# Splits, masks and bias work of a mixing layer moved from GpSimd to VectorE and ScalarE, and the input weights held in four smaller buffers

## The chip, the cores and the metric

The kernel runs on one core of a Trainium2 chip. The metric is device time in microseconds (us) of one launch, taken by a counter of the chip; a profiled execution of the same program gives the trace. The engines are named PE (TensorE, matmuls), DVE (VectorE), ACT (ScalarE), POOL (GpSimd) and SP (SyncE, which here issues most DMAs). PEld is the weight load of TensorE.

## The reference, cut to what matters

One layer on x of 256 tokens by 1024: a mixing sublayer and a top-4-of-32 mixture of experts, both with a residual and a layer norm.

```python
x = layer_norm(x, ln_in_w, ln_in_b)
p = x @ w_in                                   # 1024 x D_IN: columns of RWKV-7 (8 heads of 64) and GLA (4 heads)
p_rwkv = p_rwkv + (shift(p_rwkv) - p_rwkv)*mu   # mixes each token with the one before
decay, a, g = small two-step projections of p_rwkv
kk = k*k_k / norm(k*k_k);  k = k*(1 + (a - 1)*k_a)
S_t = S_{t-1}(diag(w_t) - kk_t (kk_t*a_t)^T) + v_t k_t^T ;  y_t = S_t r_t     # by chunks of 64 tokens
y = (groupnorm(y)*gn_w + gn_b + sum(r*k*r_k)*v) * g
o = gla_chunked(q, k, v, gk); o = rms(o)*norm_w * silu(g_gla)
x = layer_norm(alpha*x + concat(y, o) @ w_out)
# experts: 4 of 32 per token, blocks of rows sorted by expert
h = xt[tok] @ w1[e] + b1[e];  act = (clip(up) + 1)*min(gt, 7)*sigmoid(1.702*gt);  o = act @ w2[e] + b2[e]
x = layer_norm(alpha*x + sum_of_gated(o))
```

Matmuls of the mixing sublayer are to be as good as float32, so both operands are split into a high and a low part in TensorE's rounded float32 (fp32r), and three products are added.

## The kernel before, in words

The tokens lie in two tiles of 128. After the first layer norm, x is transposed and split into `xth` and `xtl`. The columns of `w_in` come in 14 blocks of up to 256 columns (8 KB in each partition); `load_win` issues each block's DMA on SP. Two blocks share one 16 KB buffer of the pool `ring` (tag `slot`, two buffers).

`split()` (lines 383 to 392) makes the two parts of a piece of 128x512 weights: `whi` by a ScalarE copy (L388), `wlo` by a subtract (L391) on the engine that is passed in, VectorE by default. `proj_t` (transposed output) and `proj_n` (output with tokens on partitions) then issue three matmuls for each weight tile (L401 to L403 in `proj_t`). The results lie in PSUM banks with the tag `p`, of which there are two. `shift` (L429 ACT, L430 DVE) takes a result out and mixes it with the token before; only then is its half of a bank free.

The order of work is found when the program is built: a scheduler places each instruction on its engine's queue by data dependence and a priority that follows the source order. Each engine then runs its queue in order, so an instruction that waits holds up all behind it.

From some 108 us on, the projections for GLA (`wqk`, `wgv`, `wgg`) run between the chunk algebra of RWKV: `scores` (L630), `inverse16` (L648 to L671: eight masked products `dgm`, L661, four by DVE from the high part and four by POOL from the low part, for each of two chunk pairs; then a serial loop of 15 steps of two small DVE instructions, L669 and L670), `doubling` (L692 to L698) and `rwkv_chunk`. POOL also scales the residual `xres` by the first norm's weight and bias (L378, four of 128x1024), multiplies the bonus term (L817) and prepares the expert bias `b1`: the 32x2048 bias lies four times on the 128 partitions and is taken apart into bf16 pieces, copy (L587), subtract (L589), copy (L590). The pieces `b1p` are the moving operand of the bias matmul L1314, with `e32b` picking the expert's row of each piece.

Then comes the out projection with `w_out`, the second norm, the router, and the experts. The expert stream has ten buffers of 16 KB: six `xp` (0 to 5, which earlier hold activations), two of `ring` ('a', the same as the two of `w_in`) and two of `ringb` ('b', opened when the pools of the mixing stage close). `fetch` issues the stream's DMAs on SP in the order given by `ORDER`, each when its buffer is free: four loads of `w_out` of 1 MB (two to a buffer), then for every pair of experts eight of `w1` and four of `w2`, 2 MB each.

Of the kernel before, what the change touches and what calls it, by code (L numbers as in the profile page):

```python
# [18 lines left out]
T = 256  # L19
# [43 lines left out]
def _pack(i):  # L63
# [47 lines left out]
    put("e32", ((p % 32) == np.arange(32)[None, :]) & (p // 32 != 1))  # L111
# [19 lines left out]
SPL = {9: (0, 0), 39: (1, None), 44: (None, 0)}  # L131

PAIRS = ((1, 7), (4, 11), (8, 9), (6, 10), (2, 5), (3, 12))
ORDER = ['a', 'b', 0, 'a', 'b', 1, 2, 3, 4, 5]
# [3 lines left out]
def mix_moe(ctx: ExitStack, tc: tile.TileContext, A, out, dbg=None):  # L138
# [9 lines left out]
    NA, NB, NX = 2, 2, 6  # L148
    NS = NA + NB + NX
    base = ctx.enter_context(tc.tile_pool(name="base", bufs=1, side="left"))  # L150
    xp = ctx.enter_context(tc.tile_pool(name="xp", bufs=1, side="left", reuse_waits="tile"))
    ring = ctx.enter_context(tc.tile_pool(name="ring", bufs=NA, side="left"))
# [32 lines left out]
    b1p = base.tile([128, 2048], BF16, name="b1p")  # L185
    e32b = base.tile([128, NE], BF16, name="e32b")
# [36 lines left out]
    wtile = [None]  # L223

    def load_win(b):
        if b % 2 == 0:
            wtile[0] = ring.tile([128, 4096], F32, name="slot", tag="slot")
        w = wtile[0][:, 2048 * (b % 2):2048 * (b % 2) + 2048]
        n = 8 * cols[b]
        o = int(woff[b])  # L230
        parts = 2 if b == 0 else 1
        for i in range(parts):
            c = slice(i * n // parts, (i + 1) * n // parts)
            nc.sync.dma_start(w[:, c], A["win"][:, o + c.start:o + c.stop])
        return w[:, :n].rearrange("p (k c) -> p k c", k=8)
# [35 lines left out]
    def fetch(n):  # L271
        while len(loaded) < min(n, len(stream)):
            i = len(loaded)
            src = stream[i]
            o = order[i % NS]
            if o in ("a", "b"):
                w = (ring if o == "a" else ringb).tile([128, 4096], F32, name="slot", tag="slot")
            else:
                w = wide(o)
            at = 0  # L280
            for r in src:
                m = math.prod(r.shape[1:])
# [20 lines left out]
    s8 = slot(8)  # L303
    lniw, lnib = cut(s8, 0, D), cut(s8, D, D)
# [4 lines left out]
    b1f = y.rearrange("p a c -> p (a c)")  # L309
    for i in range(4):  # L310
        nc.sync.dma_start(b1f[32 * i:32 * i + 32, :], A["b1"])
# [64 lines left out]
    for bc, op in ((lniw, OP.mult), (lnib, OP.add)):  # L376
        for t in range(2):
            G.tensor_tensor(xres[:, t, :], xres[:, t, :], bc, op=op)  # L378

# [33 lines left out]
    def proj_n(blocks, pss):  # L413

        for j, w in enumerate(blocks):
            for kh in range(4):
                hi, lo = split(w[:, 2 * kh:2 * kh + 2, :], [128, 2, 256], (G, V)[kh % 2])
                for t in range(2):
                    o = pss[t][:, j * 256:(j + 1) * 256]
                    for k in range(2):  # L420
                        kk = 2 * kh + k
                        ts = slice(t * 128, (t + 1) * 128)
                        PE.matmul(o, lhsT=xth[:, kk, ts], rhs=hi[:, k, :], start=(kk == 0), stop=False)
                        PE.matmul(o, lhsT=xth[:, kk, ts], rhs=lo[:, k, :], start=False, stop=False)
                        PE.matmul(o, lhsT=xtl[:, kk, ts], rhs=hi[:, k, :], start=False, stop=(kk == 7))
# [133 lines left out]
    for p in range(4):  # L559
        V.tensor_scalar(k2[:, p, :], ta[:, p, :], hka[:, p:p + 1], oka[:, p:p + 1], op0=OP.mult, op1=OP.add)  # L560
# [25 lines left out]
    G.tensor_copy(e32b, C("e32"))  # L586
    G.tensor_copy(b1p, b1f)  # L587
    for r in (64, 96):
        G.tensor_tensor(b1f[r:], b1f[r:], b1p[r:], op=OP.subtract)  # L589
        G.tensor_copy(b1p[r:], b1f[r:])  # L590
# [49 lines left out]
    def inverse16(c2):  # L640
# [16 lines left out]
        for g in range(4):  # L657
            pb = bank(RS[c2])
            for i, (d, eng) in enumerate(((hi.bitcast(F32), V), (dgf, G))):
                m = p1.tile([128, 4, 128], F32R, name="dgm", tag="xz", bufs=4)  # L660
                eng.tensor_tensor(m, d.unsqueeze(1).to_broadcast([128, 4, 128]),  # L661
                                  i16[:, 4 * g:4 * g + 4].unsqueeze(2).to_broadcast([128, 4, 128]), op=OP.mult)
                PE.matmul(pb, lhsT=ones16, rhs=m.rearrange("p b f -> p (b f)"), start=(i == 0), stop=(i == 1))
# [130 lines left out]
    for p in range(2):  # L794
        proj_t(wqk[0], p * 128, pb[:, p * T:(p + 1) * T], G)
# [3 lines left out]
    for p in range(2):  # L799
        proj_t(wqk[1], p * 128, pb[:, p * T:(p + 1) * T], G)  # L800
# [7 lines left out]
    for t in range(2):  # L808
# [435 lines left out]
    for e2 in range(NE // 2):  # L1244
# [56 lines left out]
        for i in range(2):  # L1301
# [140 lines left out]
```

## Time and profile before

| What | Value |
|---|---|
| Median of three runs | 1199.7 us (1198.8 to 1199.85) |
| Profiled execution | 1194.37 us, span 1192.5 us, clock 0.98 |
| PE busy | 1092.7 us, 92% of the span |
| DVE busy | 391.3 us, 33% |
| ACT busy | 200.6 us, 17% |
| POOL busy | 83.9 us, 7% in 75 instructions |
| DMA | 428.68 MB, mean 359 GB/s |

Up to about 243 us the mixing sublayer, the second norm and the router run; after that the experts. An engine's share of the span says little about a stage: DVE is busy for a third of the whole span, yet in the stretch from 115 to 149 it is busy nearly all the time, as a row below shows. Busy time counts an instruction from its start to its end in the trace.

### The profile page before, as it was taken

The page shows a single profiled execution, that of the slowest core. Times are in us where ns is not written, and L with a number is a line of the kernel's source. Part 1 is how long each engine was busy: PE and PEld are TensorE (multiplying, and loading weights), DVE is VectorE, ACT ScalarE, POOL GpSimd, SP SyncE. Part 2 cuts the span into 40 slices and gives each one's busy share as a digit, 9 for nine tenths or more (in the row PEclk, how much of TensorE's full clock was granted, in tenths as well). Part 3 has the DMA queues.
Part 4 walks back from the last instruction along what each step waited for, and adds up shares of the span by engine and source line. Part 5 has one row for each costly group of instructions (what it writes and reads, how often), then busy time and mean ns, then how long its engine had stood idle before and what let it go on. Part 6 is the DMA issues. An engine that isn't in the chain of part 4 may idle for free.

```text
span 1192.5 us, 14141 instructions
## 1 busy us (share of the span) xinstructions
PE 1092.7 (92%) x5964; PEld 528.8 (44%) x5964; DVE 391.3 (33%) x792; ACT 200.6 (17%) x368; POOL 83.9 (7%) x75
## 2 busy tenths in 40 slices
PE   8889899999999999999899999999899999998995
PEld 5679787643434343433333333333333333333443
DVE  7767976424222221221212222212222222222125
ACT  5544322111011111110101010110101010101111
POOL 4605610010000000000000000000000000000001
PEclk9879999998999999999999999999999999999998
DMA  9211364689799999999989999999999999999991
GB/s 336 115 71 72 142 255 166 249 346 428 285 429 428 428 429 427 427 428 429 425 357 430 425 429 429 427 426 428 429 428 428 427 428 427 428 426 428 426 400 43
DMA packets 36201, 428.68 MB, mean 359 GB/s; under 512 B 3947, under 2 KB 6276, under 8 KB 9382
## 3 DMA queue, kind: packets, MB, share of 16 engines
q1 hardware_dynamic: 35362, 426.41, 85.5%
q10 hardware_dynamic: 772, 1.32, 0.3%
q8 instruction: 48, 0.79, 0.3%
q14 instruction: 19, 0.16, 0.0%
HBM read 426.67 MB, written 1.05 MB: 359 GB/s over the span
## 4 chain that ended last, share of the span: by engine, by line
PE 28%; DMA 19%; DVE 2%; ACT 1%; issue 0%; DVEq 0%; ACTq 0%
DMA slot<-w 19%; PE bg L1310 13%; PE bo L1332 5%; PE bx L1264 4%; PE bx L1339 3%; DVE oc L1335 1%; PE bx L1368 1%; ACT oc L1334 1%; PE bx L1363 1%; PE bo L1363 1%; PE bx L1090 0%; PE bx L1286 0%; PE bx L1217 0%; DVE y L1391 0%; PE bg L1314 0%
## 5 line engine op out<-in xcount | busy, mean ns | idle before, releaser
L1310 PE MATMUL bg<-slot,xg 128*64 128x512 f32 x2048 | 462.0, 596 | 0.0
L1310 PEld LDWEIGHTS bg<-slot,xg 128*64 128x64 f32 x2048 | 140.7, 137 | 250.8 <-issue 236.2
L1332 PE MATMUL bo<-slot,aT 128*64 128x512 f32 x960 | 218.4, 601 | 35.0 <-DVE oc L1335 16.3
L1332 PEld LDWEIGHTS bo<-slot,aT 128*64 128x64 f32 x960 | 68.1, 138 | 168.4 <-issue 114.8
L1082 DVE TENSOR_SCALAR gt<-bg 128x512 f32<-128x512 f32 x32 | 22.1, 691 | 284.7 <-PE bg L1314 284.7
L1264 PEld LDWEIGHTS bx<-so,xres 128*128 128x128 f32 x512 | 67.8, 196 | 49.4 <-issue 46.4
L1335 DVE COPY oc<-bo 64x512 f32<-64x512 f32 x30 | 20.8, 694 | 205.2 <-ACT oc L1334 205.1
L1264 PE MATMUL bx<-so,xres 128*128 128x128 f32 x512 | 79.4, 292 | 1.1 <-DVEq L1121 1.1
L1100 DVE TENSOR_SCALAR xg<-bx,cst 128x128 f32<-128x128 f32 x64 | 26.2, 410 | 162.0 <-PE bx L1264 111.6
L1339 PE MATMUL bx<-oc,sgT 128*128 128x512 f32 x120 | 55.5, 605 | 21.3 <-DVE oc L1335 21.3
L1083 ACT ACTIVATE up<-gt 128x512 f32<-128x512 f32 x32 | 20.1, 629 | 312.1 <-DVE gt L1082 312.1
L1410 POOL TENSOR_TENSOR y<-y,xres 128x512 f32<-128x512 f32 x1 | 1.4, 1442 | 917.9 <-ACT y L1409 917.9
L1099 ACT ACTIVATE xg<-bx,cst 128x128 f32<-128x128 f32 x64 | 28.6, 457 | 173.8 <-PE bx L1264 170.8
L401 PE MATMUL bp<-xth,whi 128*128 128x256 f32 x144 | 45.0, 313 | 6.9 <-DVE slot L430 6.9
L1340 DVE TENSOR_TENSOR y<-bx,y 128x512 f32<-128x512 f32 x60 | 41.5, 692 | 25.8 <-PE bx L1339 25.8
L1334 ACT ACTIVATE oc<-bo 64x512 f32<-64x512 f32 x30 | 17.7, 591 | 186.9 <-PE bo L1332 179.5
L403 PE MATMUL bp<-xth,wlo 128*128 128x256 f32 x144 | 43.7, 305 | 3.6 <-DVE wlo L391 3.6
L1339 PEld LDWEIGHTS bx<-oc,sgT 128*128 128x128 f32 x120 | 21.6, 189 | 56.0 <-DVE oc L1335 34.5
L402 PE MATMUL bp<-xtl,whi 128*128 128x256 f32 x144 | 43.5, 303 | 0.0
L391 DVE TENSOR_TENSOR wlo<-slot,whi 128x512 fp32r<-128x512 f32 x37 | 35.7, 974 | 19.0 <-ACT whi L388 18.9
L388 ACT ACTIVATE whi<-slot 128x512 fp32r<-128x512 f32 x50 | 31.2, 629 | 49.6 <-PE bp L402 27.2
L1092 ACT ACTIVATE aT<-bx 128x512 f32<-128x512 f32 x32 | 19.1, 597 | 121.5 <-PE bx L1090 121.4
(419 smaller groups left out, 1020.6 us busy)
## 6 DMA issues: line engine op xcount, KB each, us to landing
slot<-w SPq DMA_DIRECT2D x188, 2048.0 KB, 34.1
slot<-win SPq DMA_DIRECT2D x12, 1024.0 KB, 7.8
slot<-w2l SPq DMA_DIRECT2D x7, 1024.0 KB, 33.2
slot<-wout SPq DMA_DIRECT2D x4, 1024.0 KB, 7.6
slot<-win SPq DMA_DIRECT2D x3, 512.0 KB, 6.8
slot<-lora SPq DMA_DIRECT2D x1, 1024.0 KB, 11.0
slot<-rows SPq DMA_DIRECT2D x2, 512.0 KB, 13.9
y<-b SPq DMA_DIRECT2D x4, 256.0 KB, 13.2
```

What stands on the lines that cost most here:

```text
L388: S.activation(hi, src, AF.Copy)
L391: (eng if b is None else (V, G)[b]).tensor_tensor(lo, src, hi.bitcast(F32), op=OP.subtract)
L401: PE.matmul(ps, lhsT=hi[:, k, :], rhs=xth[:, kk, :], start=(kk == 0), stop=False)
L402: PE.matmul(ps, lhsT=hi[:, k, :], rhs=xtl[:, kk, :], start=False, stop=False)
L403: PE.matmul(ps, lhsT=lo[:, k, :], rhs=xth[:, kk, :], start=False, stop=(kk == 7))
L1264: i = PE.matmul(pb[:, j * 128:(j + 1) * 128], lhsT=xres[:, t, c0:c0 + 255:2], rhs=so[:, t].rearrange("p a b -> p (a b)"), start=(t == 0), ...
L1310: PE.matmul(pp[64 * hf:64 * hf + 64, :], lhsT=lt, rhs=w[:, c0 + 512 * hf:c0 + 512 * hf + 512], start=(k == 0), stop=False)
L1332: PE.matmul(po[64 * half:64 * half + 64, :], lhsT=aTs[i][:, j, 64 * hf:64 * hf + 64], rhs=w[:, c0:c0 + 512], start=(f == 0), stop=(f == 7))
L1334: S.activation(oc[0:64, i, :], po[0:64], AF.Copy)
L1335: V.tensor_copy(oc[64:, 1 - i, :], po[64:])
L1339: PE.matmul(pb, lhsT=sgT[:, g, t * 128:(t + 1) * 128], rhs=oc[:, g, :], start=True, stop=True)
L1340: V.tensor_tensor(y[:, t, g * 512:(g + 1) * 512], pb, y[:, t, g * 512:(g + 1) * 512], op=OP.add)
```

## The change

1. The low part of every split is made by DVE: `proj_t` and `proj_n` no longer name POOL, and two of the three exceptions in `SPL` are gone.
2. All eight masks of each `inverse16` are made by DVE.
3. The scaling of `xres` and the bonus term go from POOL to DVE; the `xres` lines now stand in the source just ahead of the bonus, and their operand has its own tile `lni`.
4. `k2 = ta*hka + oka` (four of 128x256) goes from DVE to ACT.
5. The expert bias is loaded once, its 2048 columns spread over four groups of 32 partitions; ACT copies (three of 128x512) and DVE subtracts (two) make three bf16 pieces, and twelve DMAs on ACT's queue put them on 96 partitions. `e32b` has 96 rows and the bias matmul has 96 instead of 128 rows to sum over.
6. `w_in` has four buffers of 8 KB, one block each. `ring` closes with the mixing stage's pools; the expert stream then has its four buffers b0 to b3 in `ringb`, at the places in `ORDER` where 'a', 'b', 'a', 'b' stood.
7. The pool of scratch for dynamic DMAs is set to 1024.

```diff
-    put("e32", ((p % 32) == np.arange(32)[None, :]) & (p // 32 != 1))
+    put("e32", (p % 32) == np.arange(32)[None, :])
-SPL = {9: (0, 0), 39: (1, None), 44: (None, 0)}
+SPL = {9: (0, 0)}
-ORDER = ['a', 'b', 0, 'a', 'b', 1, 2, 3, 4, 5]
+ORDER = ['b0', 'b1', 0, 'b2', 'b3', 1, 2, 3, 4, 5]
...
-    ring = ctx.enter_context(tc.tile_pool(name="ring", bufs=NA, side="left"))
+    ring_ctx, ring = open_pool("ring", "left")
...
-        if b % 2 == 0:
-            wtile[0] = ring.tile([128, 4096], F32, name="slot", tag="slot")
-        w = wtile[0][:, 2048 * (b % 2):2048 * (b % 2) + 2048]
+        w = ring.tile([128, 2048], F32, name="slot", tag=f"w{(b + 2) % 4}")
...
-    b1f = y.rearrange("p a c -> p (a c)")
+    b1f = p1.tile([128, 512], F32, name="b1f")
+    b1s = p1.tile([128, 3, 512], BF16, name="b1s")
     for i in range(4):
-        nc.sync.dma_start(b1f[32 * i:32 * i + 32, :], A["b1"])
+        nc.sync.dma_start(b1f[32 * i:32 * i + 32, :], A["b1"][:, 512 * i:512 * i + 512])
...
-    for bc, op in ((lniw, OP.mult), (lnib, OP.add)):
-        for t in range(2):
-            G.tensor_tensor(xres[:, t, :], xres[:, t, :], bc, op=op)
...
-                hi, lo = split(w[:, 2 * kh:2 * kh + 2, :], [128, 2, 256], (G, V)[kh % 2])
+                hi, lo = split(w[:, 2 * kh:2 * kh + 2, :], [128, 2, 256])
...
-        V.tensor_scalar(k2[:, p, :], ta[:, p, :], hka[:, p:p + 1], oka[:, p:p + 1], op0=OP.mult, op1=OP.add)
+        S.activation(k2[:, p, :], ta[:, p, :], AF.Identity, scale=hka[:, p:p + 1], bias=oka[:, p:p + 1])
...
-    G.tensor_copy(e32b, C("e32"))
-    G.tensor_copy(b1p, b1f)
-    for r in (64, 96):
-        G.tensor_tensor(b1f[r:], b1f[r:], b1p[r:], op=OP.subtract)
-        G.tensor_copy(b1p[r:], b1f[r:])
+    G.tensor_copy(e32b, C("e32")[0:96])
+    for r in range(3):
+        S.activation(b1s[:, r], b1f, AF.Copy)
+        if r < 2:
+            V.tensor_tensor(b1f, b1f, b1s[:, r], op=OP.subtract)
+        for i in range(4):
+            nc.scalar.dma_start(b1p[32 * r:32 * r + 32, 512 * i:512 * i + 512], b1s[32 * i:32 * i + 32, r])
...
-            for i, (d, eng) in enumerate(((hi.bitcast(F32), V), (dgf, G))):
+            for i, (d, eng) in enumerate(((hi.bitcast(F32), V), (dgf, V))):
...
-        proj_t(wqk[0], p * 128, pb[:, p * T:(p + 1) * T], G)
+        proj_t(wqk[0], p * 128, pb[:, p * T:(p + 1) * T])
-        proj_t(wqk[1], p * 128, pb[:, p * T:(p + 1) * T], G)
+        proj_t(wqk[1], p * 128, pb[:, p * T:(p + 1) * T])
...
+    for bc, op in ((lniw, OP.mult), (lnib, OP.add)):
+        for t in range(2):
+            V.tensor_tensor(xres[:, t, :], xres[:, t, :], bc, op=op)
     for t in range(2):
...
-            G.tensor_tensor(add[hs].rearrange("p (h c) -> p h c", c=64),
+            V.tensor_tensor(add[hs].rearrange("p (h c) -> p h c", c=64),
...
     gp_ctx.close()
+    ring_ctx.close()
     p1_ctx.close()
-    ringb = ctx.enter_context(tc.tile_pool(name="ringb", bufs=NB, side="left", reuse_waits="tile"))
+    ringb = ctx.enter_context(tc.tile_pool(name="ringb", bufs=1, side="left", reuse_waits="tile"))
+    for i in range(NB):
+        ringb.tile([128, 4096], F32, name="slot", tag=f"b{i}")
...
-                PE.matmul(pp[64 * hf:64 * hf + 64, :], lhsT=e32b[:, e:e + 1].to_broadcast([128, 64]),
+                PE.matmul(pp[64 * hf:64 * hf + 64, :], lhsT=e32b[:, e:e + 1].to_broadcast([96, 64]),
...
-    nc = bacc.Bacc("TRN2", target_bir_lowering=False, num_devices=1)
+    nc = bacc.Bacc("TRN2", target_bir_lowering=False, num_devices=1, dynamic_dma_scratch_size=1024)
```

How the queues of three places read before and after; a row is line, operation, output and inputs with shape, and line numbers of the changed kernel are some 7 lower. First VectorE's queue in the second block of `w_in`, before:

```order
L391 TENSOR_TENSOR wlo<-slot,whi 128x512
L430 SCALAR_TENSOR_TENSOR slot<-bp,cst,slot 32x255
L391 TENSOR_TENSOR wlo<-slot,whi 128x512
L430 SCALAR_TENSOR_TENSOR slot<-bp,cst,slot 128x255
L454 TENSOR_SCALAR slot<-slot 32x256
L459 TENSOR_SCALAR slot<-slot 128x256
L391 TENSOR_TENSOR wlo<-slot,whi 128x512
L493 TENSOR_SCALAR slot<-slot 128x512
L390 CAST whi<-slot 128x512
L493 TENSOR_SCALAR slot<-slot 128x512
L391 TENSOR_TENSOR wlo<-slot,whi 128x512
```

and the same place after (L384 is the subtract L391 of before, L423 the shift L430, L486 the row L493):

```order
L423 SCALAR_TENSOR_TENSOR slot<-bp,cst,slot 32x255
L811 TENSOR_TENSOR xres<-xres,lni 128x1024 x2
L384 TENSOR_TENSOR wlo<-slot,whi 128x512
L423 SCALAR_TENSOR_TENSOR slot<-bp,cst,slot 128x255
L447 TENSOR_SCALAR slot<-slot 32x256
L811 TENSOR_TENSOR xres<-xres,lni 128x1024
L486 TENSOR_SCALAR slot<-slot 128x512
L811 TENSOR_TENSOR xres<-xres,lni 128x1024
L583 TENSOR_TENSOR b1f<-b1f,b1s 128x512
L486 TENSOR_SCALAR slot<-slot 128x512
L384 TENSOR_TENSOR wlo<-slot,whi 128x512
L452 TENSOR_SCALAR slot<-slot 128x256
```

The four scalings of `xres` (L811) and the first bias subtract (L583) now stand between the splits on VectorE.

Second, VectorE's queue at the masks of the first `inverse16`, before:

```order
L430 SCALAR_TENSOR_TENSOR slot<-bp,cst,slot 128x255
L655 CAST dgs<-dg 128x128
L656 TENSOR_TENSOR dg<-dg,dgs 128x128
L661 TENSOR_TENSOR dgm<-dgs,cstm 128x512 x2
L630 TENSOR_TENSOR slot<-bs,cstm 128x4x128
L661 TENSOR_TENSOR dgm<-dgs,cstm 128x512 x2
L796 SCALAR_TENSOR_TENSOR slot<-bp,slot 128x512
L669 TENSOR_TENSOR tp<-y,xd 128x8x2
```

and after (L656 is the mask L661, L625 the row L630):

```order
L650 CAST dgs<-dg 128x128
L651 TENSOR_TENSOR dg<-dg,dgs 128x128
L656 TENSOR_TENSOR dgm<-dgs,cstm 128x512
L384 TENSOR_TENSOR wlo<-slot,whi 128x512
L656 TENSOR_TENSOR dgm<-dg,cstm 128x512
L656 TENSOR_TENSOR dgm<-dgs,cstm 128x512
L656 TENSOR_TENSOR dgm<-dg,cstm 128x512
L384 TENSOR_TENSOR wlo<-slot,whi 128x512
L656 TENSOR_TENSOR dgm<-dgs,cstm 128x512
L625 TENSOR_TENSOR slot<-bs,cstm 128x4x128
L656 TENSOR_TENSOR dgm<-dg,cstm 128x512
L384 TENSOR_TENSOR wlo<-slot,whi 128x512
```

The four masks of the low part stand among the four of the high part, with the splits of the GLA projections between them. (L669 and what follows it come later than these rows.)

Third, ScalarE's queue where k's norm and GLA's decay are made, before (L614 and L615 are the two exponentials that read one `p` bank, L241 the square root of `rsqrt`):

```order
L429 ACTIVATE slot<-bp,par 128x256
L614 ACT_TABLE_LOAD
L614 ACTIVATE slot<-bp 128x512
L241 ACT_TABLE_LOAD
L241 ACTIVATE rsu<-ssn 128x16
L388 ACTIVATE whi<-slot 128x512 x2
L429 ACTIVATE slot<-bp,par 128x256
L388 ACTIVATE whi<-slot 128x512
L539 ACTIVATE ivT<-ba 8x256
L615 ACT_TABLE_LOAD
L615 ACTIVATE enc<-bp 128x512
L388 ACTIVATE whi<-slot 128x512
```

and after (L609 and L610 are the two exponentials, L237 the square root, L553 the moved `k2`):

```order
L381 ACTIVATE whi<-slot 128x512
L553 ACTIVATE slot<-slot,par 128x256 x4
L237 ACT_TABLE_LOAD
L237 ACTIVATE rsu<-ssn 128x16
L381 ACTIVATE whi<-slot 128x512
L422 ACTIVATE slot<-bp,par 128x256
L609 ACT_TABLE_LOAD
L609 ACTIVATE slot<-bp 128x512
L381 ACTIVATE whi<-slot 128x512 x2
L422 ACTIVATE slot<-bp,par 128x256
L532 ACTIVATE ivT<-ba 8x256
L610 ACTIVATE enc<-bp 128x512
```

One table load fewer stands there (two instead of three), four activations more, and the second exponential follows the first without a table load between.

## Rows read from the trace of the kernel before

**Rows 1.** the page's chain that ended last, shares of the span by line

```profile
DMA slot<-w 19%; PE bg L1310 13%; PE bo L1332 5%; PE bx L1264 4%; PE bx L1339 3%; DVE oc L1335 1%; PE bx L1368 1%; ACT oc L1334 1%; PE bx L1363 1%; PE bo L1363 1%; PE bx L1090 0%; PE bx L1286 0%; PE bx L1217 0%; DVE y L1391 0%; PE bg L1314 
```

**Rows 2.** busy time in four stretches; columns: us, engines' busy (instructions), PEclk, DMA, GB/s

```profile
20.00:62.00 42.00, 34.86 (x211) 27.92 (x210) 32.90 (x30) 24.03 (x48) 26.46 (x12) 0.92 0.45 149
...
108.00:115.00 7.00, 7.00 (x55) 6.57 (x54) 5.99 (x8) 4.82 (x9) 6.49 (x7) 1.00 0.01 4
...
115.00:149.00 34.00, 28.31 (x258) 27.06 (x256) 32.95 (x58) 13.13 (x22) 22.48 (x17) 0.95 0.33 125
...
610.00:1150.00 540.00, 499.56 (x2356) 195.36 (x2354) 113.00 (x214) 57.66 (x105) 0.00 (x0) 1.00 1.00 424
```

**Rows 3.** the chain late in the expert stage; start us, us, what

```profile
773.63 35.79 DMA slot<-w
```

**Rows 4.** TensorE's timeline, four waits from 20 to 92 [idle before <- releaser]

```profile
24.70 0.70 PE L483 MATMUL br<-slot 64*128 64x256 f32 x2 [1.01 <-DVE slot L430]
...
35.84 0.58 PE L403 MATMUL bp<-xth,wlo 128*128 128x256 f32 x1 [3.59 <-DVE wlo L391]
...
60.25 0.39 PE L401 MATMUL bp<-xth,whi 128*128 128x256 f32 x1 [2.54 <-DVE slot L430]
...
77.23 0.58 PE L401 MATMUL bp<-xth,whi 128*128 128x256 f32 x1 [3.85 <-DVE slot L430]
```

**Rows 5.** the stretches at a low granted clock, columns as in rows 2

```profile
34.40:41.20 6.80, 5.37 (x17) 3.86 (x18) 6.80 (x7) 0.63 (x1) 5.88 (x3) 0.51 0.01 1
...
61.80:65.20 3.40, 3.40 (x19) 3.40 (x18) 1.73 (x4) 2.40 (x5) 0.00 (x0) 0.50 0.00 0
...
75.50:82.30 6.80, 5.07 (x23) 4.92 (x24) 2.83 (x7) 1.01 (x3) 2.55 (x1) 0.50 0.00 0
```

**Rows 6.** VectorE's timeline, four of its instructions from 28 to 60

```profile
28.43 6.35 DVE L454 TENSOR_SCALAR slot<-slot 32x256 f32<-32x256 f32 x1
...
35.71 0.41 DVE L493 TENSOR_SCALAR slot<-slot 128x512 f32<-128x512 f32 x1
...
36.38 4.29 DVE L493 TENSOR_SCALAR slot<-slot 128x512 f32<-128x512 f32 x1
...
54.12 5.68 DVE L391 TENSOR_TENSOR wlo<-slot,whi 128x512 fp32r<-128x512 f32 x2 [0.75 <-ACT whi L388]
```

**Rows 7.** GpSimd's timeline, two of its instructions in the same stretch

```profile
35.10 5.29 POOL L589 TENSOR_TENSOR y<-y,b1p 64x2048 f32<-64x2048 f32 x1
...
52.50 4.45 POOL L589 TENSOR_TENSOR y<-y,b1p 32x2048 f32<-32x2048 f32 x1
```

**Rows 8.** ScalarE's timeline and its queue (ACTq)

```profile
68.69 1.28 ACT L614 ACT_TABLE_LOAD   x1
...
83.59 0.60 ACT L615 ACTIVATE enc<-bp 128x512 f32<-128x512 f32 x1
...
240.07 0.34 ACTq L1238 DMA_DIRECT2D b2t<-b  x1
```

**Rows 9.** GpSimd by line; columns: xcount | busy, mean ns | idle before, releaser

```profile
L391 POOL TENSOR_TENSOR wlo<-slot,whi 128x512 fp32r<-128x512 f32 x15 | 20.6, 1379 | 28.4 <-ACT whi L388 28.3
...
L661 POOL TENSOR_TENSOR dgm<-dg,cstm 128x512 fp32r<-128x512 f32 x8 | 10.2, 1276 | 10.5 <-PE bs L663 7.6 <-DVE tp L669 2.9
```

**Rows 10.** VectorE by line and shape from 108 to 172.6, columns as before

```profile
L391 DVE TENSOR_TENSOR wlo<-slot,whi 128x512 fp32r<-128x512 f32 x9 | 9.1, 1006 | 0.0
...
L661 DVE TENSOR_TENSOR dgm<-dgs,cstm 128x512 fp32r<-128x512 f32 x8 | 8.5, 1079 | 1.0 <-PE br L663 1.0
...
L822 DVE TENSOR_TENSOR slot<-slot,gnw 128x512 f32<-128x512 f32 x2 | 3.4, 1702 | 0.0
...
L820 DVE TENSOR_TENSOR y<-y,gnb 128x512 f32<-128x512 f32 x2 | 3.0, 1524 | 0.0
...
L669 DVE TENSOR_TENSOR tp<-y,xd 128x96 f32<-128x96 f32 x1 | 1.1, 1122 | 0.0
```

**Rows 11.** VectorE by line and shape from 173 to 243, GpSimd idle

```profile
L857 DVE TENSOR_TENSOR yc<-yc,r 128x512 f32<-128x512 f32 x2 | 1.4, 691 | 0.0
```

More of the change, by code (lines that the diff above doesn't have):

```diff
@@ L146, in open_pool @@
         return c, p
-    NA, NB, NX = 2, 2, 6
-    NS = NA + NB + NX
+    NB, NX = 4, 6
+    NS = NB + NX
     base = ctx.enter_context(tc.tile_pool(name="base", bufs=1, side="left"))
     xp = ctx.enter_context(tc.tile_pool(name="xp", bufs=1, side="left", reuse_waits="tile"))
-    ring = ctx.enter_context(tc.tile_pool(name="ring", bufs=NA, side="left"))
+    ring_ctx, ring = open_pool("ring", "left")
     ps_ctx = ExitStack()
@@ L184, in mix_moe @@
     rb = base.tile([128, NE], F32, name="rb")
-    b1p = base.tile([128, 2048], BF16, name="b1p")
-    e32b = base.tile([128, NE], BF16, name="e32b")
+    b1p = base.tile([96, 2048], BF16, name="b1p")
+    e32b = base.tile([96, NE], BF16, name="e32b")
     def C(name):
@@ L221, in mix_moe @@
     woff = np.concatenate([[0], np.cumsum([8 * c for c in cols])])
-    wtile = [None]
     def load_win(b):
-        if b % 2 == 0:
-            wtile[0] = ring.tile([128, 4096], F32, name="slot", tag="slot")
-        w = wtile[0][:, 2048 * (b % 2):2048 * (b % 2) + 2048]
+        w = ring.tile([128, 2048], F32, name="slot", tag=f"w{(b + 2) % 4}")
         n = 8 * cols[b]
@@ L275, in fetch @@
             o = order[i % NS]
-            if o in ("a", "b"):
-                w = (ring if o == "a" else ringb).tile([128, 4096], F32, name="slot", tag="slot")
+            if isinstance(o, str):
+                w = ringb.tile([128, 4096], F32, name="slot", tag=o)
             else:
@@ L302, in mix_moe @@
     wk.append(load_win(3))
-    s8 = slot(8)
-    lniw, lnib = cut(s8, 0, D), cut(s8, D, D)
+    lni = p1.tile([128, 2, D], F32, name="lni")
+    lniw, lnib = lni[:, 0], lni[:, 1]
     row_bcast(lniw, "lniw", nc.sync)
```

## The prediction

> **What bounds the kernel now.** I read the page's chain first. It ends in the expert stage: 19% of the span is a wait for expert weights [rows 1], and late in the stage the chain is one wait after another like the 35.79 us at 773.63 [rows 3]. From 610 to 1150 the DMA engines are full, 1.00 at 424 GB/s [rows 2]. So from the point where the stream runs the end is fixed by bytes, and nothing that PE saves there moves it. What moves it is when the stream gets going: its buffers come free as the mixing stage ends and the first experts are computed. A microsecond saved ahead of the experts therefore moves the end by a microsecond, as long as the first weights are there in time.
>
> Then I read the mixing stage by windows [rows 2]. From 108 to 149 DVE is busy 5.99 + 32.95 = 38.9 of 41 us, PE 35.3: this part is bound by VectorE. From 20 to 62 PE is busy 34.9 of 42, and its timeline gives waits of 1.01, 3.59 and 2.54 us, each ended by a DVE instruction, and one of 3.85 after 73 [rows 4]. After the three long ones the granted clock falls to half for 3.4 or 6.8 us [rows 5]; after the one of 1.01 it doesn't, so such a wait costs more than itself.
>
> Why is DVE late? The timelines show it. A TENSOR_SCALAR of 32x256 took 6.35 us at 28.43; one of 128x512 took 4.29 where its twin took 0.41 [rows 6]. The 4.29 one ends at 40.67, and GpSimd's bias subtract of 5.29 ends at 40.39 [rows 7]. The two splits at 54.12 (5.68 for a pair that should take 2 x 0.69 = 1.4) run beside GpSimd's subtract of 4.45 [rows 6, 7]. With GpSimd idle a 128x512 takes 0.69 [rows 11]. So VectorE is held up while GpSimd works.
>
> The Trainium skill, "SBUF — State Buffer", section "SBUF: two separate sides", has this as a lock: a GpSimd instruction and a VectorE instruction with two SBUF inputs, or in a two-port mode, take a shared pair of ports in turn, each for its whole length. The end times above agree.
>
> **The change part by part.** All sums are against the profiled execution, 1194.37 us, which is 5.3 below the median of 1199.7.
>
> A1, 20 to 46. The wait of 1.01 goes, since its DVE shift no longer stands behind stretched splits. For the wait of 3.59: before, from 28.43 DVE runs the 6.35, a TENSOR_SCALAR (0.41) and the split (0.69), 7.5. After, between the same shift and the same split stand L447 and two L486 (3 x 0.41), two scalings of 128x1024 (twice a 128x512 each: 2.8), a bias subtract and the split (2 x 0.69): 5.4 [rows 6, 11]. That is 2.1 less, and two scalings more stand ahead, where stretched splits stood; these I count as even. Of the 3.59 some 1.7 is left. The half clock behind it cost about half of its busy 5.37, so 2.7 [rows 5]; a wait of 1.7 lies between 1.01, after which the clock held, and 2.54, after which it didn't, so I take four tenths back, 1.1. A1 = 1.0 + 1.9 + 1.1 = 4.0; bounds 1 and 7 (all waits and the clock).
>
> A2, 46 to 66. No GpSimd bias work is left: the splits at 54.12 are 4.3 shorter, more than the wait of 2.54, and the half clock after it cost half of 3.40 [rows 4 to 6]. 2.5 + 1.7 = 4.2; taken 4.0, bounds 2 and 4.2.
>
> B, 66 to 92. The wait of 3.85 and two low-clock stretches (half of 5.07, and half of a fourth stretch of 3.40 like the second, from 85.7 on) are worth 3.85 + 2.5 + 1.7 = 8.0 [rows 4, 5]. Its cause before: one of the two `p` banks is held from the exponential behind the table load at 68.69 to the second one at 83.59 [rows 8], so the projections have one bank and every block waits for its shift, which stands behind the norm's algebra on DVE. After, the two exponentials are close in ScalarE's queue. But PE now meets the norm's transpose and broadcast in this place too, and ScalarE has four more activations (k2, at most 0.6 each) ahead of the square root that this chain waits for. I take 3.5, nearer to the middle; bounds -1.7 (the wait stays and the clock falls once more) and 8.0.
>
> The Trainium skill, "ScalarE: Activation LUTs", section "What ACT_TABLE_LOAD costs", puts a table switch at about 2.66 us with its drain. The row shows 1.28, and the activation follows at once. By the page the one switch saved would be worth 1.4 more in B; I keep the row.
>
> C, 92 to 108. In PE's new order the chunk algebra begins some 44 projection matmuls earlier, each 0.11 (28.31 by 258) [rows 2]: the same work in another order. Taken 0, bounds 0 and 4.8 (if the scalar loop behind it starts that much earlier and DVE has room).
>
> D, 108 to 173, the part that DVE bounds and the one against the change. Off DVE: over all its instructions here, each against the same shape with GpSimd idle, I count 16.8 us of stretch. The rows carry its bulk: splits 9 x (1.006 - 0.69) = 2.8, masks 8 x (1.079 - 0.69) = 3.1, L822 2 x 1.01, L820 2 x 0.83, and the loop's small products, of which one of 128x96 took 1.12 [rows 10, 11]. On DVE: 11 of GpSimd's 15 splits, 8 masks and 4 bonus products fall here, and two splits that others made: 25 x 0.65 = 16.3. GpSimd took 1379 and 1276 ns for such splits and masks [rows 9], but those times are not on DVE's queue. Net about nothing; taken -1 (a loss), since the moved masks now stand in one queue with what PE waits for. Bounds: +6 (waits for GpSimd's masks go as well) and -8 (half of the stretch stays).
>
> By the skill's lock the stretch could be as long as GpSimd's own busy time, 6.49 + 22.48 = 29.0 from 108 to 149 [rows 2], and the stage would give up to 12 more, 1177. The rows bear 16.8, which I keep.
>
> ScalarE takes three copies of 0.60, the four k2 and twelve DMA issues of 0.34 [rows 8], 8 us in all. It is busy 24 of 42 us from 20 to 62 [rows 2] and waits for PE, which hides them; each issue waits for its copy with the next `whi` copy behind it, so without that cover perhaps 2 are lost. Taken 0. The DVE bias subtract waits for ScalarE's copy, with L486 and a split behind it; counted in A1 without wait. The w_in loads on SP now wait for one block's splits instead of two, so they come earlier if at all; no PE wait in the rows is for them. The bias matmul has the same columns, and the expert stage waits for DMA anyway. The expert buffers keep their places in the stream's order. All taken 0.
>
> Sum: 4.0 + 4.0 + 3.5 + 0 - 1 = 10.5. 1194.4 - 10.5 = 1183.9 in the profiled execution, and 1199.7 - 10.5 = 1189 for the median.
>
> **The rivals.**
> 1. More comes back: B in full (+4.5), C half (+2.4), and the clock in A1 (+1.6), 8.5 more: 1181. For it: each of these hangs on one or two waits. Against: B's chain through norm and table is still there, and it needs several at once.
> 2. The end doesn't follow: the first experts wait for weights or router instead, and the time stays at 1199.7. For it: DMA is full later. Against: the ten buffers' first loads are long done when the experts start, and SP issues the later ones only as buffers come free.
> 3. Slower: VectorE becomes the bound of 108 to 173. GpSimd's stretch has only partly to do with the moved work; if half of the 16.8 returns, 8.4 stands against 16.3, a loss of 8. With B giving nothing and A1 and A2 together 4, the time is 1199.7 + 4 = 1204. The point from which it decides: with A at 8 and B at 0, less than 16.3 - 8 = 8.3 returning. For it: DVE is busy 38.9 of 41 there. Against: the stretch follows GpSimd's instructions in time [rows 6, 7].
>
> **How the numbers follow.** Two tenths of a per cent, 2.4 us, is about what a measurement can tell from no change. The forecast, 0.62, has its own range of 1184 to 1196 by A1 and B at their bounds. Rival 1, 0.18, reaches 1179 with D's upper side. Rival 2, 0.07, is no change; rival 3, 0.13, lies above, a little of it near no change. Faster 0.80, same 0.08, slower 0.12. The range of 1179 to 1200 leaves out most of rival 3 and the far end of rival 1, under 2 in 10.
>
> **What would show it.** Right: no DVE instruction of 128x512 over 1 us before 173; PE's waits at 24.7 and 60.3 gone, the one at 35.8 below 2; the granted clock whole from 55 to 66; DVE's busy from 108 to 173 about the same in more instructions; the experts' first matmul some 10 us earlier. Wrong: DVE still stretched with GpSimd idle, a PE wait for masks or for ScalarE's copies, or an earlier start of the experts that the end doesn't follow.

## The result, and the profile after

The changed kernel takes 1183.7 us (median of four, 1183.28 to 1185.44), before 1199.25 (median of four, 1193.3 to 1199.85). The ratio is 0.9884, 95% interval 0.9851 to 0.9917: faster, by 10 to 18 us. The forecast was 1189, the range 1179 to 1200. The profiled execution after takes 1183.28 us with a span of 1181.1. Before it took 1194.37 with a span of 1192.5, so between the two profiles lie 11.1 us (11.4 in the span), against 10.5 in the sum.

The chain late in the expert stage is as it was, only earlier (start, length, what; answers to [rows 3]):

```profile
762.23 35.99 DMA slot<-w
```

Busy time after in three stretches (length, then each engine's busy time with its instructions, the granted clock, DMA share, GB/s; answers to [rows 2]):

```profile
20.00:62.00 42.00, 38.65 (x264) 32.50 (x263) 25.44 (x44) 31.18 (x61) 0.92 (x3) 1.00 0.55 190
...
98.00:131.10 33.10, 33.10 (x256) 31.17 (x255) 29.10 (x73) 18.08 (x31) 0.61 (x2) 1.00 0.18 65
...
610.00:1150.00 540.00, 499.14 (x2360) 196.51 (x2358) 113.74 (x215) 59.24 (x108) 0.00 (x0) 1.00 1.01 426
```

From 20 to 62 DVE went from 32.90 us in 30 entries to 25.44 in 44, POOL from 26.46 to 0.92, and the clock from 0.92 to whole. From 98 to 131 PE is now busy all of the time; from 108 to 149 before it was for 35.3 of 41 us. The stream from 610 on is unchanged.

TensorE's timeline after, its waits from 20 to 72 and its first expert matmul (start, length, operation, the idle time ahead and what ended it; answers to [rows 4]):

```profile
32.59 0.94 PE L493 MATMUL br<-cstm,slot 128*128 128x128 f32 x6 [0.99 <-DVE slot L486]
...
52.91 0.38 PE L394 MATMUL bp<-xth,whi 128*128 128x256 f32 x1 [1.29 <-DVE slot L423]
...
64.31 0.46 PE L394 MATMUL bp<-xth,whi 128*128 128x256 f32 x1 [3.38 <-DVE slot L423]
...
231.85 4.51 PE L1312 MATMUL bg<-slot,xg 128*64 128x512 f32 x20
```

The waits of 1.01 and 3.59 are gone; near the place of the second stands one of 0.99, for another VectorE instruction (L486). The wait of 2.54 has become 1.29, and 3.85 is still 3.38. The stretches at the low granted clock (half of full, 1.2 GHz) from 20 to 240, columns as for the windows, answer to [rows 5]:

```profile
64.50:67.90 3.40, 3.40 (x17) 3.40 (x17) 2.08 (x9) 1.52 (x3) 0.00 (x0) 0.50 0.02 5
...
71.30:78.10 6.80, 6.80 (x29) 5.96 (x28) 6.65 (x12) 0.63 (x1) 2.03 (x1) 0.50 0.41 148
...
228.30:231.70 3.40, 3.40 (x16) 3.39 (x16) 0.93 (x4) 0.92 (x2) 0.00 (x0) 0.50 1.05 400
```

The falls behind the first two waits have gone; the ones behind 64.3 stayed, and a new one lies at 228.

VectorE's timeline after, the kinds of instruction shown before in [rows 6]:

```profile
28.72 0.27 DVE L447 TENSOR_SCALAR slot<-slot 32x256 f32<-32x256 f32 x1
...
32.13 0.41 DVE L486 TENSOR_SCALAR slot<-slot 128x512 f32<-128x512 f32 x1
...
53.70 0.69 DVE L384 TENSOR_TENSOR wlo<-slot,whi 128x512 fp32r<-128x512 f32 x1
```

The TENSOR_SCALAR of 32x256 takes 0.27 instead of 6.35, that of 128x512 takes 0.41 instead of 4.29, a split 0.69. By line and shape, the stretch that answers to 108 to 172 before (answers to [rows 10]):

```profile
L384 DVE TENSOR_TENSOR wlo<-slot,whi 128x512 fp32r<-128x512 f32 x22 | 14.9, 685 | 1.4 <-ACT whi L381 1.3
...
L656 DVE TENSOR_TENSOR dgm<-dgs,cstm 128x512 fp32r<-128x512 f32 x8 | 6.2, 774 | 0.5 <-PE br L658 0.5
...
L656 DVE TENSOR_TENSOR dgm<-dg,cstm 128x512 fp32r<-128x512 f32 x8 | 5.5, 683 | 0.0
```

In the 68 us from 92 to 160 VectorE makes 22 splits and 16 masks, where it made 9 and 8 in 64.6, at 683 to 774 ns instead of 1006 and 1079.

Where the time went is read best by four stages. Each ends with the start of one PE instruction that both kernels have, in lines of before: A from the first matmul of L401 to the last of L532 (k's norm), B to the last of L581 (bonus), C+D to the first of L989 (out projection), R to the first of L1310 (experts). A starts at 17.8 to 19.2 us, so the stages do not add up to the experts' start by themselves.

| Kernel | A | B | C+D | R | experts start | median us (runs) |
|---|---|---|---|---|---|---|
| before | 50.8 | 22.1 | 113.7 | 38.9 | 243.2 | 1199.25 (4) |
| changed | 41.4 | 20.4 | 111.3 | 40.8 | 231.9 | 1183.7 (4) |
| changed, second profile | 41.4 | 19.5 | 112.8 | 39.7 | 231.8 | 1184.8 (8) |
| bias work on GpSimd | 46.0 | 19.6 | 111.4 | 40.3 | 235.6 | 1190.1 (10) |
| residual on GpSimd | 44.6 | 20.4 | 110.9 | 39.7 | 233.9 | 1187.5 (7) |
| idle products in A | 44.2 | 19.6 | 113.4 | 39.7 | 235.3 | 1187.7 (10) |
| idle products in D | 41.4 | 19.4 | 112.9 | 39.7 | 231.8 | 1185.3 (10) |
| w_in in two buffers | 41.4 | 20.9 | 111.2 | 39.7 | 231.8 | 1182.2 (4) |
| k2 on VectorE | 41.4 | 17.5 | 111.8 | 40.9 | 229.8 | 1182.8 (4) |
| masks on GpSimd | 41.4 | 19.5 | 108.9 | 39.7 | 227.9 | 1182.3 (4) |
| splits on GpSimd | 41.4 | 19.4 | 111.2 | 38.9 | 230.0 | 1179.3 (4) |
| masks, splits on GpSimd | 41.4 | 19.4 | 117.3 | 40.8 | 236.7 | 1189.1 (10) |
| masks, splits on GpSimd, k2 on VectorE | 41.4 | 18.6 | 117.1 | 39.7 | 235.4 | 1187.7 (10) |
| masks on GpSimd, k2 on VectorE | 41.4 | 18.6 | 110.3 | 39.1 | 227.7 | 1179.7 (4) |

The kernel before, run beside the experiments, gave medians of 1195.1 to 1195.9 over 16 to 23 runs, from 1190 to 1207, so the gain by those runs is 10 to 12 us rather than 15.5.

### The profile page after: what moved, and what is told of

Same layout as the page of the kernel before. It is cut to its first block, busy times and chain, and to the rows that moved or that the text cites. A ratio compares the mean times of both kernels' runs of the same rounds, so it can differ in the third digit from the quotient of the medians.

```text
span 1181.1 us, 14146 instructions
## 1 busy us (share of the span) xinstructions
PE 1089.2 (92%) x5964; PEld 525.5 (44%) x5964; DVE 379.2 (32%) x821; ACT 202.7 (17%) x375; POOL 21.6 (2%) x38
## 4 chain that ended last, share of the span: by engine, by line
PE 28%; DMA 19%; DVE 2%; ACT 1%; issue 0%; DVEq 0%; ACTq 0%
DMA slot<-w 19%; PE bg L1312 13%; PE bo L1334 5%; PE bx L1266 4%; PE bx L1341 3%; DVE oc L1337 1%; PE bx L1370 1%; ACT oc L1336 1%; PE bx L1365 1%; PE bo L1365 1%; PE bx L1092 0%; PE bx L1288 0%; PE bx L1219 0%; DVE y L1393 0%; DVE up L1088 0%
## 5 line engine op out<-in xcount | busy, mean ns | idle before, releaser
L1334 PE MATMUL bo<-slot,aT 128*64 128x512 f32 x960 | 219.6, 605 | 33.1 <-DVE oc L1337 14.8
L1084 DVE TENSOR_SCALAR gt<-bg 128x512 f32<-128x512 f32 x32 | 22.1, 692 | 284.3 <-PE bg L1316 284.2
L1336 ACT ACTIVATE oc<-bo 64x512 f32<-64x512 f32 x30 | 17.8, 592 | 189.5 <-PE bo L1334 182.1
L384 DVE TENSOR_TENSOR wlo<-slot,whi 128x512 fp32r<-128x512 f32 x52 | 35.4, 687 | 18.3 <-ACT whi L381 18.1
L1094 ACT ACTIVATE aT<-bx 128x512 f32<-128x512 f32 x32 | 19.1, 598 | 117.1 <-PE bx L1092 117.1
L394 PEld LDWEIGHTS bp<-xth,whi 128*128 128x128 f32 x144 | 29.3, 203 | 7.5 <-DVE slot L423 5.1
```

Source lines behind the costliest of these rows:

```text
L384: (eng if b is None else (V, G)[b]).tensor_tensor(lo, src, hi.bitcast(F32), op=OP.subtract)
L394: PE.matmul(ps, lhsT=hi[:, k, :], rhs=xth[:, kk, :], start=(kk == 0), stop=False)
L1334: PE.matmul(po[64 * half:64 * half + 64, :], lhsT=aTs[i][:, j, 64 * hf:64 * hf + 64], rhs=w[:, c0:c0 + 512], start=(f == 0), stop=(f == 7))
L1336: S.activation(oc[0:64, i, :], po[0:64], AF.Copy)
```

## The experiments

The first theory: GpSimd's instructions hold VectorE's up, TensorE waits for VectorE, and its clock falls behind the wait. Its rivals: VectorE's queue is the bound and any work added to it costs; or the new order and the buffers made the gain. Each kernel starts from the changed one. In the two with idle products and in the one with the old buffers the instructions of VectorE and TensorE keep their order; in the others the scheduler moves some, so those test the move together with its new order.

**Idle products in A.**

```diff
+    for t in range(2):
+        dm = p1.tile([128, 512], F32, name="dum", tag="dum")
+        for h in range(2):
+            G.tensor_tensor(dm, xres[:, t, 512 * h:512 * h + 512], lniw[:, 0:512], op=OP.mult)
```

> The changed kernel, and four GpSimd products of 128x512 on the scaled residual, whose result nobody reads, some 30 to 36 us from the start; the other engines' order is that of the changed kernel. Theory: VectorE's subtracts and scalings there grow by up to the 5.5 us that GpSimd works, TensorE's wait of 0.99 at 32.6 becomes 3 to 6 and the granted clock falls once to half: the whole is 4 to 8 us slower. Rival: within 1 us of the changed kernel.

Measured: 1187.69 us, ratio to before 0.9925 (0.9899 to 0.9951); stage A 44.2 instead of 41.4. The timelines of GpSimd, VectorE and TensorE in it:

```profile
30.81 7.85 POOL L815 TENSOR_TENSOR dum<-xres,lni 128x512 f32<-128x512 f32 x4
...
32.05 1.76 DVE L583 TENSOR_TENSOR b1f<-b1f,b1s 128x512 f32<-128x512 f32 x1
...
35.75 1.36 DVE L452 TENSOR_SCALAR slot<-slot 128x256 f32<-128x256 f32 x1
...
34.20 0.94 PE L493 MATMUL br<-cstm,slot 128*128 128x128 f32 x6 [2.07 <-DVE slot L486]
```

The bias subtract takes 1.76 instead of 0.67 and a TENSOR_SCALAR of 128x256, which has one input, 1.36 instead of 0.28. TensorE's wait doubled to 2.07, a fall of the clock of 3.4 us followed, and 2.8 us were lost with no change but GpSimd's work. The theory holds in kind, but 4 to 8 was too much: the wait grew by 1.1 and not by 2 to 5. GpSimd's four products were held up in turn, 7.85 where 5.5 was expected.

**The bias work on GpSimd again.**

```diff
-    for r in range(3):
-        S.activation(b1s[:, r], b1f, AF.Copy)
...
+    G.tensor_copy(b1p, b1f)
+    for r in (64, 96):
+        G.tensor_tensor(b1f[r:], b1f[r:], b1p[r:], op=OP.subtract)
+        G.tensor_copy(b1p[r:], b1f[r:])
```

> The changed kernel with the expert bias taken apart by GpSimd as before (four loads of 256 KB, 15.7 us of casts and subtracts on GpSimd, 128 rows in the bias matmul). Theory (GpSimd's work holds VectorE up, and the bias work is the larger part of it from 28 to 62): waits of TensorE of 2 us and more for VectorE between 30 and 60 come back with one or two falls of the clock, the experts start 4 to 7 us later than at 231.9. Rival (the residual's scalings were the cause, and the twelve DMA issues on ScalarE's queue cost as much as the bias work): within 1 us.

Measured: 1190.06 us, ratio 0.995 (0.9923 to 0.9976); A 46.0, 4.6 more, experts 3.7 later. TensorE's waits in it:

```profile
38.50 1.10 PE L502 MATMUL br<-slot 128*128 128x512 f32 x2 [1.99 <-DVE slot L451]
...
52.38 0.39 PE L395 MATMUL bp<-xth,wlo 128*128 128x256 f32 x1 [1.95 <-DVE wlo L383]
```

Two waits of 2 us for VectorE are back, though no fall of the clock in A. So the bias work (with its loads and its 128 rows, which the edit puts back too) is worth 4.6 of the 9.4 that A gained.

**The residual's scalings on GpSimd again** (the four lines as in the kernel before, at their old place).

> The changed kernel with the four scalings of the residual on GpSimd again (9.9 us there, 4.8 less on VectorE). Theory: 2 to 5 us slower by stretched VectorE instructions from 25 to 36. Rival (VectorE's own queue is the limit there, so that giving it back helps): 1 us or more faster.

Measured: 1187.52 us, ratio 0.9921 (0.9892 to 0.995); A 44.6, 3.2 more, with the wait at 33:

```profile
33.36 0.49 PE L497 MATMUL br<-cstm,slot 128*128 128x128 f32 x2 [1.71 <-DVE slot L490]
```

and one fall of the clock behind it. As the theory had it. 4.6 and 3.2 are 7.8 of the 9.4; the two were not put back together, so that they add is not shown.

**The input weights in two buffers of 16 KB again** (`load_win`, `ring`, `ringb` and `ORDER` of before).

> The changed kernel with the input weights in two buffers of 16 KB again, two blocks in each, and the expert stream's buffers as before; the order on VectorE, TensorE and GpSimd is that of the changed kernel. Theory (the buffers earn nothing, term 0): within 1 us. Rival (the weights' earlier arrival is part of the gain): 2 us or more slower, with a wait for a load of the input weights or of the first expert weights in the profile.

Measured: 1182.15 us, ratio 0.9888 (0.9842 to 0.9935), all stages as in the changed kernel. The buffers earn nothing in time.

**k2 back on VectorE.**

```diff
-        S.activation(k2[:, p, :], ta[:, p, :], AF.Identity, scale=hka[:, p:p + 1], bias=oka[:, p:p + 1])
+        V.tensor_scalar(k2[:, p, :], ta[:, p, :], hka[:, p:p + 1], oka[:, p:p + 1], op0=OP.mult, op1=OP.add)
```

> The changed kernel with k2 back on VectorE. Theory: TensorE's wait of 3.38 at 64.3 comes from ScalarE's queue, where four k2 activations (59.0 to 61.1) and the square root's table load stand ahead of the shift; without them the wait shrinks to about 1.3 and one or both of the low-clock stretches behind it go: 2 to 6 us faster. Rival (VectorE is the limit there and takes 1.4 us more): the wait stays, 0 to 2 us slower.

Measured: 1182.75 us, ratio 0.99 (0.9853 to 0.9946). B is 17.5 instead of 20.4, and the experts start 2.1 earlier; by the end nothing of it is left (span 1181.2 against 1181.1). The first experts have 3.4 us more of low clock in this profile, which may be why. ScalarE's queue in the changed kernel:

```profile
59.01 2.08 ACT L553 ACTIVATE slot<-slot,par 128x256 f32<-128x256 f32 x4 [0.97 <-PE ba L525]
...
61.10 1.28 ACT L237 ACT_TABLE_LOAD   x1
...
63.04 0.45 ACT L422 ACTIVATE slot<-bp,par 128x256 f32<-128x256 f32 x1
```

and with k2 on VectorE, with VectorE's half of the shift (L423) and TensorE's wait:

```profile
60.80 0.46 ACT L422 ACTIVATE slot<-bp,par 128x256 f32<-128x256 f32 x1
...
61.28 1.28 ACT L237 ACT_TABLE_LOAD   x1
...
63.09 0.48 DVE L423 SCALAR_TENSOR_TENSOR slot<-bp,cst,slot 128x255 f32<-128x255 f32 x1
...
63.63 0.39 PE L394 MATMUL bp<-xth,whi 128*128 128x256 f32 x1 [2.39 <-DVE slot L423]
```

The shift's first half (L422) stood at 63.04 behind k2 and the table load; now it runs at 60.80, ahead of it. The wait shrinks by 1.0, not by the 2 of the expectation: ScalarE's half is done at 61.3, but VectorE, which now makes k2, comes to its own half only at 63.09.

**Idle products in D**: GpSimd makes the eight low masks once more, unread.

```diff
+                if i == 1:
+                    dm = p1.tile([128, 4, 128], F32R, name="dum", tag="dum")
+                    G.tensor_tensor(dm, d.unsqueeze(1)..., i16[...]..., op=OP.mult)
```

> The changed kernel, and beside it GpSimd makes the eight low masks once more into a tile that nobody reads; every other engine's order is word for word that of the changed kernel. Theory (GpSimd's work holds VectorE up): eight GpSimd products of some 1.28 us, 10.2 in all, stretch VectorE's instructions beside them, most of all its masks (0.69 in the changed kernel, 1.08 before); part is hidden, since TensorE is full from 92 to 149: the experts start 2 to 8 us later than at 231.9. Rival (what GpSimd does beside VectorE costs nothing, the gain from 92 on came from waits for GpSimd's results or from the new order): within 1 us.

Measured: 1185.34 us, ratio 0.9919 (0.9897 to 0.9941); C+D 112.9, as in the changed kernel's second profile. GpSimd and VectorE in it:

```profile
94.22 5.70 POOL L660 TENSOR_TENSOR dum<-dg,cstm 128x512 fp32r<-128x512 f32 x4 [3.05 <-DVE dg L651]
...
97.50 1.52 DVE L656 TENSOR_TENSOR dgm<-dgs,cstm 128x512 fp32r<-128x512 f32 x1
...
117.07 0.84 DVE L668 TENSOR_TENSOR tp<-y,xd 128x64 f32<-128x64 f32 x1
```

Masks took 1.52 instead of 0.69, and the loop's product of 128x64 took 0.84; the changed kernel has 0.26 for it:

```profile
115.71 0.26 DVE L664 TENSOR_TENSOR tp<-y,xd 128x64 f32<-128x64 f32 x1
```

VectorE is held up as plainly as in A, and the experts still start at 231.8: TensorE is the full engine there, and in the changed kernel VectorE was busy for 29.1 of 33.1 us, so the stretch fell into its free time. The expectation of 2 to 8 us failed, the rival's number held, though not its reason.

**The splits, then the masks, on GpSimd again**, each alone.

```diff
+SPL = {9: (0, 0), 39: (1, None), 44: (None, 0)}          # splits: and G in proj_t, (G, V)[kh % 2] in proj_n
...
+            for i, (d, eng) in enumerate(((hi.bitcast(F32), V), (dgf, G))):    # masks
```

> The changed kernel with the 15 low-part splits on GpSimd again (20.6 us there, about 10 less on VectorE). Theory: what VectorE is relieved of comes back as stretch; 0 to 4 us slower from 100 to 160, VectorE's busy time there about the same in fewer instructions. Rival (VectorE is the bound from 92 on and takes over too much): 2 us or more faster.

> The changed kernel with the eight low masks on GpSimd again (10.2 us there, 5.4 less on VectorE). Theory: 0 to 3 us slower, VectorE's masks at 1 us and more beside GpSimd's. Rival: 1 us or more faster, since VectorE has less to do.

Measured, splits: 1179.34 us, ratio 0.9852 (0.9807 to 0.9897), C+D 111.2, the same as in the changed kernel. Masks: 1182.25 us, ratio 0.988 (0.9834 to 0.9927), C+D 108.9, 2.4 to 3.9 less. In both the theory's sign failed: neither move earned its place by itself, and the masks' move cost. The splits' kernel has the same C+D and yet a span 4.1 us shorter. Of that 1.9 is there when the experts start (B is 1.0 shorter, and R is 1.9 shorter without the fall of the clock at 228), and 2.2 comes later, where its first experts ran at a higher clock. The first pair of experts in the changed kernel, and in that with the splits on GpSimd:

```profile
262.00:294.00 32.00, 28.21 (x98) 9.30 (x96) 11.11 (x19) 4.66 (x8) 0.00 (x0) 0.84 0.92 381
```

```profile
262.00:294.00 32.00, 28.32 (x103) 9.52 (x100) 11.17 (x17) 3.15 (x6) 0.00 (x0) 0.89 0.99 411
```

The stretch from 97 to 131 with the masks on GpSimd, and with the splits there:

```profile
97.00:131.00 34.00, 34.00 (x286) 32.18 (x286) 32.55 (x76) 18.59 (x31) 4.78 (x6) 1.00 0.19 63
```

```profile
97.00:131.00 34.00, 30.45 (x245) 27.96 (x246) 33.00 (x67) 14.27 (x25) 13.66 (x12) 0.95 0.18 63
```

**Masks and splits on GpSimd**, and the same with k2 on VectorE: what is left of the change in D is the bonus.

> The changed kernel with both the 15 low splits and the eight low masks on GpSimd again, as before the change; the residual, the bonus, the bias and k2 stay where the change put them. Theory (moving splits and masks earned nothing; the gain is that of the bias and residual work): the stretch from the bonus matmul to the out projection takes 108 to 112 us (111.2 in the changed kernel, 109.0 with the masks alone on GpSimd, 111.1 with the splits alone). Rival (each alone is harmless, both together hold VectorE up as before): 113 us or more, and the experts start 2 us or more later than at 231.9.

> The changed kernel with splits and masks on GpSimd and k2 on VectorE: what is left of the change is the bias, the residual, the bonus and the buffers. Theory: as fast as the changed kernel or up to 5 us faster, out projection from 186 to 190. Rival (GpSimd's work holds VectorE up from 92 on as before): out projection at 193 or later.

Measured: 1189.11 us, ratio 0.9958 (0.9933 to 0.9983), and 1187.73, ratio 0.994 (0.9918 to 0.9962); C+D 117.3 and 117.1. The rival was right, by more than it said. The first one's waits of TensorE, the bonus products on VectorE, and the stretch:

```profile
113.62 0.55 PE L416 MATMUL bp<-whi,xth 128*128 128x256 f32 x1 [2.85 <-DVE slot L791]
...
126.47 1.97 PE L674 MATMUL br<-cst,slot 64*64 64x64 f32 x32 [4.85 <-DVE slot L666]
...
120.15 5.54 DVE L816 TENSOR_TENSOR y<-slot,bon 64x512 f32<-64x512 f32 x4
...
97.00:131.00 34.00, 25.90 (x191) 23.91 (x192) 32.01 (x60) 11.95 (x21) 18.41 (x16) 0.85 0.19 63
```

Now TensorE waits for VectorE, 2.85 and 4.85 us, the second time for a product behind four bonus products that took 5.54 instead of 2.7. 10.2 us of low clock lie in C+D, where the changed kernel has none or 3.4. VectorE's busy time does not tell the three kernels apart: it is 32.6 of 34 us with the masks, 33.0 with the splits and 32.0 with both on GpSimd. In the same stretch GpSimd is busy for 4.8, 13.7 and 18.4 us, and TensorE for 34.0, 30.5 and 25.9, with 286, 245 and 191 matmuls. A stretched instruction counts as busy like any other; what decides is whether TensorE comes to wait.

With both on GpSimd, C+D takes 117, longer than the 113.7 of before. One difference in this stretch is that before had the bonus on GpSimd as well; whether the bonus products on VectorE are the cause was not tried.

**Masks on GpSimd and k2 on VectorE.**

> The changed kernel with the low masks on GpSimd and k2 on VectorE. Theory (the two gains add: 2.7 us from the masks, 2.1 from k2, read at the start of the out projection, 191.0 in the changed kernel): the out projection starts at 186 to 187.5, and the whole is 1178 to 1182. Rival (one wait takes the other's place): 188.5 or later.

Measured: 1179.68 us (1177.91 to 1180.63), ratio 0.9881 (0.9834 to 0.9928); the changed kernel beside it had 1184.82 (1183.35 to 1185.44), so the two don't overlap. The out projection starts at 188.6, on the rival's side: the two gains don't add, the masks alone had 188.3. This version beats both kernels, the changed one by 5 us, of which 4.1 are there when the experts start; the 2.6 that it is ahead of the masks alone come after that.

**The changed kernel once more.**

> The changed kernel once more, beside the three others: 1182 to 1186, the same profile; what differs is the clock's falls, so this gives how far two profiles of one kernel lie apart.

Measured: 1184.82 us, ratio 0.9901 (0.9865 to 0.9936), where 1182 to 1186 was expected. Its profile differs from the first by 1.5 in C+D and 1.1 in R, each with a fall of the clock in one and not the other. Differences of a stage below 1.5 are therefore not read as effects.

## Why the prediction was right, point by point

**The sum.** 10.5 was forecast between the profiles, 11.1 measured (1183.9 and 1183.28 us for the profiled execution). By the median the forecast is 5.3 too high, and that is the baseline: it starts from 1199.7, while the kernel before has medians of 1195.1 to 1195.9 in the larger sets of runs. That the sum fits so closely is partly luck: by the first profile A gave 1.4 more than forecast, B 1.8 less, C and D 3.4 more, and R, which had no term, took 1.9. Two slips in the working are small: 2.1 off the wait of 3.59 leaves 1.5 and not 1.7, and A1 and B at their bounds give 1181.5 to 1197 and not 1184 to 1196.

**That a gain ahead of the experts moves the end.** Right: the experts start 11.3 earlier, the span is 11.4 shorter, and the stream from 610 on is the same. Rival 2 is out.

**A1 and A2** (4.0 and 4.0). 9.4 in place of 8.0. The mechanism is shown: with idle GpSimd work alone, 2.8 come back, with the bias work 4.6, with the residual 3.2. The wait at 35.8 went altogether, with one of 0.99 near it, rather than to 1.7, and the clock held throughout. The wait in A2, which was to go, left 1.29, which cost no clock either.

**B** (3.5). Measured 1.7, and 2.6 in the second profile. The wait of 3.85 became 3.38, hardly shorter. The four k2 activations, which I named and let pass in the middle of the range, are part of the reason: with k2 on VectorE it is 2.39. With k2 on VectorE B takes 17.5 to 18.6 in three kernels, with k2 on ScalarE 19.4 to 20.9, so this part of the change cost some 1 to 3 us of B. A wait that the forecast did not have stands here too: TensorE waits 1.06 us for ScalarE's `ivT` (L532), and the longer of the two falls of the clock lies behind it. Before, no wait for ScalarE over 0.25 us lies in B; with k2 on VectorE it is 0.76.

```profile
70.21 2.32 PE L547 MATMUL ba<-ivT,slot 8*128 8x256 f32 x7 [1.06 <-ACT ivT L532]
```

**C and D** (0 and -1). This step had the wrong sign, as far as one profile of before can tell: C+D is 2.4 shorter in the first profile, 0.9 in the second, and 0.9 is less than two profiles of one kernel differ by. VectorE's busy time came out as forecast: from the bonus to the out projection it is 88.9 us before and 89.3 after, in more instructions. What I had not counted is that a stretched instruction costs where TensorE stands behind it: TensorE's waits over 0.25 us there fell from 8.9 to 5.6 in sum, and 6.8 us of low clock went. The reverse is as true: the extra stretch of the idle masks cost nothing. Putting back splits and masks together costs 4.5 to 6 us of C+D; putting back one of them costs nothing or gains. So the sum of stretches says little, and the prediction's first reading, that a VectorE busy for 38.9 of 41 us bounds the stretch, doesn't follow from its busy time either: with the masks on GpSimd it is busy for 32.6 of 34 us and TensorE for all of them. TensorE's waits say it.

**Rival 3** (VectorE becomes the bound). Not so here, since TensorE is full from 98 to 131, but the gain from giving the masks back shows that the change went further than it had to.

**ScalarE's copies and issues** (0). Right for A. The issues took longer than the 0.34 of [rows 8]:

```profile
27.95 0.60 ACTq L585 DMA_DIRECT2D b1p<-b1s  x1
```

but TensorE waits for no ScalarE copy in A. The weights' buffers (0): right, shown by the old ones. The 96 rows of the bias matmul and the bonus products were not tried apart.

**The other signs.** Of VectorE's 128x512 instructions from 20 to 173 us one still takes over 1 us, a mask of 1.40 at 142.42, while GpSimd works. The clock was to be whole from 55 to 66; it falls at 64.5, since B now starts earlier.

**R.** Not foreseen: 1.9 us are lost in the first profile, which has a fall of the clock at 228, behind a wait of 1.03 for the router that before has too. The second profile, without that fall, loses 0.8.

The rule of the Trainium skill, "SBUF — State Buffer", section "SBUF: two separate sides", that the two engines take the shared ports in turn, agrees with the idle products in A: VectorE's subtract grew from 0.67 to 1.76, and GpSimd's four products took 7.85. The 1177 that the prediction worked out from it wasn't reached; the idle masks show a reason, since a held-up engine costs only where it is waited for.

## What to carry to other kernels

Before moving work between VectorE and GpSimd, read for each stretch which engine TensorE waits for: where TensorE waits for VectorE, GpSimd's work beside it costs time through waits and clock (in A 2.8, 3.2 and 4.6 us for 7.6, 10.4 and 18.4 us more of GpSimd's busy time), and where it doesn't (the idle masks in D), the experts start no later. VectorE's busy share doesn't tell the two cases apart. Move the part that meets the wait, and stop there; here the bias, the residual and either the splits or the masks were enough (the bonus was moved in every kernel tried). An idle copy of the moved work, which leaves every other queue in its order, tells this apart from the scheduler's reordering.

## What the runs showed of the hardware that was not expected

Kernels with more of GpSimd's work tend to spread more: 1183.3 to 1185.4 for the changed kernel over both sets of runs, 1186 to 1195 with splits and masks on GpSimd, 1187 to 1195 with the bias work there, 1190 to 1207 before. It is no rule: the splits on GpSimd gave 1178.5 to 1181.4 in four runs. Why was not tried.

The rest of the time goes with the granted clock in the first experts; which of the two causes the other was not tried. From the first expert matmul to the end of the span the three profiles with 6.8 us of low clock between 240 and 300 took 947.0 to 949.6 us, the four with 9.5 to 10.2 took 949.1 to 949.6, the seven with 13.7 took 950.6 to 952.9. The kernels near 1179 are two of the three; so some us of a comparison of whole times can be this. Two profiles of the changed kernel alone differ by 1.5 us there.
